# A two-layer decoder trunk on one core: norm steps in PSUM, four squares summed by TensorE, and four plain blocks in layer 1's second group

## The chip, the cores and the metric

The kernel runs on one core of a Trainium2 chip. The metric is the device time of one execution in microseconds (us). The core has a matrix engine (TensorE, PE in the profile, with PEld for its weight loads), a vector engine (VectorE, DVE), an activation engine (ScalarE, ACT), GpSimd (POOL) and SyncE (SP), which issues most of the DMA transfers. Each engine works through its own queue in order and waits there on semaphores of the others.

## The reference

One inference step of a trunk of two layers for 1024 prompt tokens and 64 sample tokens (8 requests of 8), all with the same weights. Model width is 1024, the channel mixer is 2816 wide, everything is float32.

```
for layer in (0, 1):
    hn  = rms_norm(h, norm_mix_g[layer])
    mix = conformer + stick-breaking attention   (layer 0)
          short gated convolution + causal pooling (layer 1)
    h   = h + mix
    g, u = split(rms_norm(h, norm_ffn_g[layer]) @ w_ffn_in[layer])
    h   = h + (silu(g) * u) @ w_ffn_out[layer]
y = rms_norm(h, norm_final_g)
rms_norm(x, g) = x * rsqrt(mean(x*x) + 1e-6) * g
```

Beside y, the new keys, values and convolution states are returned. The change lies in the norms and in layer 1's channel mixer (the last lines).

## The kernel before

**Layout and groups.** Activations are kept transposed: `hb` is [128, 8, 1088], 8 chunks (`n` or `k`) of 128 channels by 1088 token columns. Group A (`GA`) is columns 0 to 511 and four tiles of 128 tokens, group B (`GB`) is columns 512 to 1087 and five tiles (t = 4 to 8, the last half full). Every f32 product is made of three float32r products (high by high, high by low residual, low by high), so weights are split on the way in: ACT copies the high part (L187, L199), POOL subtracts it for the low part (L189, L200). `w_next` takes the next split weight tile `hl` (three buffers) and keeps the split up to two tiles and the loads up to four `stage` buffers ahead; SP issues the loads in the order of the list `seq`.

**Order of work.** The schedule is written by hand: each engine's queue has the order in which the Python emits. Side work is given out in slots between products: `slot()` is called at points inside a block and runs a step of a generator or pops a closure from a list.

**The norm.** `add_squares` squares a chunk on ACT (L254) and adds it to `ss` on POOL (L255); the first chunk is squared straight into `ss`. `norm_cols` lets TensorE add over the channels (L262: one token tile of `ss` is the weight, a column of ones the moving operand; each appears as two records), ACT takes the square root (L267), and DVE makes one Newton step for the reciprocal root with small [128, tiles] operations (L268 to L273) through the SBUF tiles `nw` and `rstd`. `norm_a` then multiplies an identity by `rstd` into `dg` (L279), `norm_b` spreads it over rows with a product by ones (L288) and ACT copies it to `rr` (L289).

**The channel mixer of layer 1.** `channel1` runs `run_ffn` for group A, then for group B. Each handles 22 column blocks f of 128 of the gate and the up half. The first `PLAIN1[group]` blocks are plain: `one(f, 0)` and `one(f, 1)`, each with 8 x 3 x 2 = 48 products of 288 columns for group B, 96 for the two. The others are done by `strassen(f)` with seven half-size products, 84 matmuls (L540) and additions on DVE (L544); four split weight tiles serve one f (sums of weight quarters on DVE, L203 to L205 and L217). In group A an output tile (`out_tile`, 24 matmuls of 512 columns at L238) follows each Strassen block from f = 2 on. Before: `PLAIN1 = (0, 1)`, so group A has no plain block and group B has one f, two plain blocks.

**The operands of the Strassen form.** They are combinations of quarters of the normed activations. For group A `forms_a` makes them while the mixer's output product of group B runs (`for n in range(KC)` with `block(GB, ...)` and `out_fin(GB, n, a)`, which adds to `hb` at L300 and calls `add_squares`). For group B `forms_b` is a generator run at every third slot of group A's channel blocks: `norm_a` at slot 3, `norm_b` at slot 9, and then the normed chunks into four tiles `xs[k]` (L1736). Once group A's products are done, `free_a` fills two lists:

- `seam`: eight pieces (ACT copy at L1840 and a low part on DVE at L1739, put off by the list `lowq`) and then the first two `job`s; `go_on` pops them in the slots of group A's last output products (`out_both`).
- `jobs`: the other two jobs, popped at every third slot of group B's plain blocks. `ready` runs what is left before the first Strassen block.

A `job(k)` makes four differences (L1743), three ACT copies (L1862) and three low parts (L1739). `last_part` cuts the last quarters after `out_both`. In group B's later slots `rows_a` squares, norms and writes group A's result. `to_y` and `finish` do the last output products of group B, its final norm in two parts (`norm_cols` for tiles 4 and 5, then 6 to 8 with `last7`) and the output.

Of the kernel before, what the change touches and what calls it, by code (L numbers as in the profile page):

```python
# [8 lines left out]
F = mybir.dt.float32  # L9
FR = mybir.dt.float32r  # L10
I32 = mybir.dt.int32
AF = mybir.ActivationFunctionType
OP = mybir.AluOpType
# [3 lines left out]
D = 1024  # L17
# [7 lines left out]
EPS = 1e-6  # L25
# [4 lines left out]
def f32(ap):  # L30
    return ap.bitcast(F)
# [14 lines left out]
GA = Grp(0, HALF, (0, 1, 512, 0))  # L46
GB = Grp(HALF, T, (0, 2, 288, 0))
# [10 lines left out]
def trunk_kernel(ctx, tc, x_prompt, x_sample, cache_k, cache_v, state_conformer, state_shortconv, state_pool,  # L58
# [4 lines left out]
    pe, act, dve, pool, sp = nc.tensor, nc.scalar, nc.vector, nc.gpsimd, nc.sync  # L63

    consts = ctx.enter_context(tc.tile_pool(name="consts", bufs=1))
# [12 lines left out]
    def tmp():  # L78
        return tmpbox[0].tile([128, tmpbox[1]], F, name="tmp")
# [4 lines left out]
    ones = consts.tile([128, 128], F, name="ones")  # L84
    dve.memset(ones, 1.0)
    eps = consts.tile([128, 1], F, name="eps")
# [3 lines left out]
    ss = consts.tile([128, 1152], F, name="ss")  # L90
    pool.memset(ss, 0.0)
    rr = consts.tile([128, T], F, name="rr")
    rstd = consts.tile([128, 9], F, name="rstd")
    nw = consts.tile([128, 2, 9], F, name="nw")
    hb = hpool.tile([128, KC, T], F, name="hb")
    park = dram.tile([128, KC, T], F, name="park")

# [39 lines left out]
            add_out(w_ffn_out[l], NF // 2 - 1, o)  # L137


    PLAIN, PLAIN1 = 5, (0, 1)  # L140


    EVEN = [(j, c) for c in range(4) for j in (0, 1, 2, 3)] + [(4, c) for c in range(4)]
# [105 lines left out]
    def add_squares(g, src, first):  # L249
        if first:  # L250
            act.activation(ss[:, g.cs], src, AF.Square)
            return
        t = tmp()
        act.activation(t[:, :g.n], src, AF.Square)  # L254
        pool.tensor_tensor(ss[:, g.cs], ss[:, g.cs], t[:, :g.n], op=OP.add)  # L255


    def norm_cols(ps, count, t0, t1, more=None):
        m = ps()
        c = slice(t0, t1)  # L260
        for t in range(t0, t1):
            pe.matmul(m[:, t:t + 1], ss[:, t * 128:t * 128 + 128], ones[:, 0:1], start=True, stop=more is None)  # L262
            if more is not None:
                pe.matmul(m[:, t:t + 1], more[:, (t - t0) * 128:(t - t0) * 128 + 128], ones[:, 0:1], start=False,
                          stop=True)
        r = rstd[:, c]
        act.activation(r, m[:, c], AF.Sqrt, bias=eps, scale=1.0 / count)  # L267
        dve.tensor_scalar(nw[:, 0, c], m[:, c], 1.0 / count, EPS, op0=OP.mult, op1=OP.add)  # L268
        dve.reciprocal(r, r)

        dve.tensor_tensor(nw[:, 1, c], nw[:, 0, c], r, op=OP.mult)
        dve.scalar_tensor_tensor(nw[:, 1, c], nw[:, 1, c], -0.5, r, op0=OP.mult, op1=OP.mult)
        dve.scalar_tensor_tensor(r, nw[:, 1, c], 1.5, r, op0=OP.add, op1=OP.mult)  # L273

    def norm_a(g, ps, count, dg=None):
        norm_cols(ps, count, g.t0, g.t1)
        k = g.t1 - g.t0
        dg = tmp() if dg is None else dg
        dve.tensor_tensor(dg[:, :k * 128].rearrange("p (t n) -> p t n", t=k),  # L279
                          ident[:, None, :].to_broadcast([128, k, 128]),  # L280
                          rstd[:, g.t0:g.t1, None].to_broadcast([128, k, 128]), op=OP.mult)
        return dg

    def spread(g, ps, src, scale):
# [6 lines left out]
    def norm_b(g, ps, dg):  # L291
        spread(g, ps, dg, 1.0)
# [5 lines left out]
    def added(g, dst, acc):  # L298
        for a, d in parts(g, acc, dst):
            dve.tensor_tensor(d, a, d, op=OP.add)  # L300
# [75 lines left out]
    lowq = []  # L376

    def low(n=0):
        while len(lowq) > n:
            lowq.pop(0)()  # L380
# [286 lines left out]
    def accs():  # L667
        return accbox["p"].tile([128, len(accbox["g"].blocks), 512], F, name="acc")

    def ms():  # L670
        return mp.tile([128, 512], F, name="m")
# [37 lines left out]
    m = ms()  # L709
# [838 lines left out]
    with tc.tile_pool(name="hid0b", bufs=2) as hidp:  # L1548
        fstack = ExitStack()
        fp = sums["p"] = fstack.enter_context(tc.tile_pool(name="forms", bufs=1))  # L1550
        forms, jobs = make_forms(GB, fp, FFNG)
# [178 lines left out]

    def out_fin(g, n, a):
        added(g, hb[:, n, g.cs], a)
        add_squares(g, hb[:, n, g.cs], n == 0)

    def normed(out, c, cs, view=lambda ap: ap):
        dve.scalar_tensor_tensor(out, view(hb[:, c, cs]), pc(FFNG + 8 + c), view(rr[:, cs]), op0=OP.mult, op1=OP.mult)  # L1736

    def lows(o, src):
        dve.tensor_tensor(o[:, 1], src, f32(o[:, 0]), op=OP.subtract)  # L1739

    def sums_t(b11, b12, b21, b22, t1, t2, t3, t4):
        for o, p, q in ((t1, b12, b11), (t3, b22, b12), (t2, b22, t1), (t4, b21, t2)):
            dve.tensor_tensor(o, p, q, op=OP.subtract)  # L1743
# [36 lines left out]
    a0, a1 = pair(GA, accs, xa, KS, {})  # L1780
    w_split(wj[0] + 3)
    out_fin(GA, 0, a0)
    out_fin(GA, 1, a1)
    todo_b = list(KS)

# [5 lines left out]
    for n in range(2, KC):  # L1791
        h = w_next()
        a = accs()
# [4 lines left out]
    with tc.tile_pool(name="fab", bufs=1) as ep:  # L1798
        gen = forms_a(ep)
        for n in range(KC):  # L1800
            h = w_next()
            a = accs()
# [14 lines left out]
    xs = [fp.tile([128, 2 * GB.n], F, name=f"xs{k}") for k in range(4)]  # L1817
    L, R = slice(0, W2), slice(W2, GB.n)
    seam, jobs, rest_b = [], [], {}


    def forms_b():
        dg = norm_a(GB, ms, D, xs[3])
        yield 1
        yield 1
        norm_b(GB, ms, dg)
        yield 1
        for k in range(4):
            normed(xs[k][:, 0:GB.n], k + 4, GB.cs)
            yield 1  # L1830
            normed(xs[k][:, GB.n:], k, GB.cs)
            yield 1

    def parts_b(k):
        return [xs[k][:, i * W2:i * W2 + W2] for i in range(4)]


    def free_a():
        def piece(o, i):
            act.activation(o[:, 0], i, AF.Copy)  # L1840
            low(1)
            lowq.append(lambda: lows(o, i))

        for k in range(4):
            seam.append(lambda k=k: piece(b2[k], xs[k][:, 0:GB.n]))
            seam.append(lambda k=k: piece(b1[k], parts_b(k)[2]))


        def last_part(k):
            if k == 0:  # L1850
                rest_b["t"] = hidp1.tile([128, 2, 2, GB.n], FR, name="hid").rearrange(
                    "p a s (b n) -> p (a s) b n", b=2)
            piece(rest_b["t"][:, k], parts_b(k)[3])

        def job(k):
            low()
            b21, b22, b11, b12 = parts_b(k)
            fast = k < 2
            t3 = b12 if k > 1 else fp.tile([128, W2], F, name="t3", bufs=2)
            sums_t(b11, b12, b21, b22, b11, b22, t3, b21)  # L1860
            for o, x in ((xa[k], xs[k][:, W2:3 * W2]), (xa[4 + k][:, :, R], t3), (xa[4 + k][:, :, L], b21)):
                act.activation(o[:, 0], x, AF.Copy)  # L1862
                if fast:
                    lowq.append(lambda o=o, x=x: lows(o, x))
                else:
                    lows(o, x)

        jobs.extend(lambda k=k: job(k) for k in range(4))
        seam.extend(jobs.pop(0) for _ in range(2))
        rest_b["f"] = last_part  # L1870

    def go_on():
        if len(lowq) > 2 or not seam:
            low(max(len(lowq) - 1, 0))
        elif seam:
            seam.pop(0)()
# [5 lines left out]
    def channel1(g, last, side, free, plain, x):  # L1882
        side = side()
        turn[0] = 0
        j0 = wj[0]

        def slot():
            turn[0] += 1
            if seam:
                return go_on()  # L1890
            if jobs and g is GB:
                if turn[0] % 3 == 0:
                    jobs.pop(0)()
            elif turn[0] % 3 == 0:
                if g is GA or wj[0] > j0 + 2 * plain + 2:
                    next(side, 0)

        def end(hh):
            if g is GB:
                for _ in side:  # L1900
                    pass
                fstack.close()
            last(hh)

        run_ffn(g, accs, ms, hidp1, x, end, slot=slot, forms=dict(form_views(g.n // 2), ready=ready), plain=plain,
                free=free, hw=GB.n, both=g is GA)
# [38 lines left out]
    def to_y(hh):  # L1945
# [44 lines left out]
        last7 = yp.tile([128, 384], F, name="last7")  # L1990
# [6 lines left out]
                sp.dma_start(y_p[0, t * 128:t * 128 + 128], y[:, t - 4])  # L1997

        def finish():
            norm_cols(ms, D, 6, 9, last7)  # L2000
            for t in range(6, 9):
                r = slice(0, 128 if t < 8 else 64)
                if t % 2:
                    act.activation(y[r, t - 4], y[r, t - 4], AF.Copy, scale=rstd[r, t:t + 1])
                else:
                    dve.tensor_scalar(y[r, t - 4], y[r, t - 4], rstd[r, t:t + 1], None, op0=OP.mult)
                if t < 8:
                    sp.dma_start(y_p[0, t * 128:t * 128 + 128], y[:, t - 4])
                else:
                    sp.dma_start(y_s.rearrange("b q c -> (b q) c"), y[:64, 4])  # L2010

        LAG = 2
        for q in range(16 + LAG):
# [6 lines left out]
            if q == 10:  # L2020
                norm_cols(ms, D, 4, 6)
        finish()

    channel1(GB, to_y, rows_a, lambda: None, PLAIN1[1],
# [40 lines left out]
```

## Time and profile before

| | |
|---|---|
| median of 3 runs | 2494.81 us (2493.42 to 2498.12) |
| profiled execution | 2494.09 us, its span 2492.3 us |
| TensorE busy (matmul) | 2415.4 us, 97% |
| DVE, ACT, POOL busy | 1625.9, 1104.3, 1617.5 us |
| granted TensorE clock, mean | 0.996 |

The span goes from the first to the last instruction. A row of a timeline is: start in us, length in us, engine, line of the source, operation, output<-inputs, shapes, count; in brackets the idle time of the engine before the row and what ended it. A busy TensorE row is modelled and says little of its speed, so starts are compared with starts. A group or tile row gives min/median/max or mean in ns. Rows of the chain that ended last are: start, length, engine, tile, line and count.

### The profile page before, as it was taken

To read this page: it belongs to the slowest core of one execution; us is meant where nothing else is said; L and a number is where in the kernel's file an instruction comes from. 1 tells how busy PE (TensorE), PEld (TensorE's weight loads), DVE (VectorE), ACT (ScalarE), POOL (GpSimd) and SP (SyncE) were. 2 spreads that over 40 slices of the span, in tenths; PEclk is the share of its full clock that TensorE was granted. 3 is DMA by queue.
4 is the path that set the end of the run, shared out by engine and by line. 5 is a ranking of instruction groups with operands and counts; after the bars stand their busy time and mean duration, and the time that the engine had idled before them with its cause. 6 is when DMAs were issued, how large, how long until landed. Compare 5 with 4: busy or idle time off the path is not lost.

```text
span 2492.3 us, 41476 instructions
## 1 busy us (share of the span) xinstructions
PE 2415.4 (97%) x15877; PEld 2188.2 (88%) x15877; DVE 1625.9 (65%) x2288; ACT 1104.3 (44%) x1877; POOL 1617.5 (65%) x1264
## 2 busy tenths in 40 slices
PE   8999999999999999999999999998999999999998
PEld 6788977788777679999999999888889988999998
DVE  3696878977777553766566533457666668666655
ACT  5535877754444343443333422234343344443333
POOL 6664344655554576787787523277888886887775
PEclk9999999999999999999999999999999999999999
DMA  7332241234665524223232311252333332233322
GB/s 224 113 109 75 76 123 43 72 111 137 179 181 169 161 90 152 77 69 100 87 98 85 113 52 43 61 150 62 92 102 102 100 96 85 85 102 113 92 85 81
DMA packets 355486, 258.32 MB, mean 104 GB/s; under 512 B 22913, under 2 KB 303617, under 8 KB 355272
## 3 DMA queue, kind: packets, MB, share of 16 engines
q1 hardware_dynamic: 355256, 255.66, 34.7%
q8 instruction: 126, 2.06, 0.3%
q14 instruction: 72, 0.59, 0.1%
q10 hardware_dynamic: 32, 0.01, 0.0%
HBM read 237.41 MB, written 18.69 MB: 103 GB/s over the span
## 4 chain that ended last, share of the span: by engine, by line
PE 75%; DVE 13%; POOL 5%; ACT 4%; issue 3%; DMA 1%; SPq 0%; DVEq 0%; ACTq 0%; POOLq 0%
PE acc L238 44%; PE acc L540 22%; POOL hl L200 2%; DVE q L1035 1%; DVE hb L300 1%; PE o L1057 1%; PE m L1159 1%; PE z L1182 1%; PE m L1047 1%; DVE cacc L858 1%; PE z L1018 1%; POOL hl L189 1%; DVE be L1037 1%; DVE sum L203 1%; DVE hid L244 1%
## 5 line engine op out<-in xcount | busy, mean ns | idle before, releaser
L189 POOL TENSOR_TENSOR hl<-stage,hl 128x512 fp32r<-128x512 f32 x464 | 638.6, 1400 | 391.6 <-ACT hl L187 279.9
L238 PE MATMUL acc<-x,hl 128*128 128x512 f32 (+1 forms) x3648 | 771.2, 349 | 11.3 <-DVE tmp L296 3.0
L238 PEld LDWEIGHTS acc<-x,hl 128*128 128x128 f32 x3648 | 585.6, 189 | 74.9 <-issue 5.8
L238 PE MATMUL acc<-hid,hl 128*128 128x288 f32 (+1 forms) x3096 | 542.1, 331 | 5.3 <-DVE hb L300 2.1
L238 PEld LDWEIGHTS acc<-hid,hl 128*128 128x128 f32 x3096 | 468.3, 189 | 51.0 <-DVE hb L300 4.2
L540 PE MATMUL acc<-x,hl 128*128 128x288 f32 (+1 forms) x2676 | 367.9, 291 | 7.9 <-POOL hl L200 3.7
L300 DVE TENSOR_TENSOR hb<-acc,hb 128x512 f32<-128x512 f32 (+1 forms) x360 | 255.5, 718 | 169.9 <-PE acc L238 168.6
L540 PEld LDWEIGHTS acc<-x,hl 128*128 128x128 f32 x2676 | 352.2, 189 | 14.1 <-POOL hl L200 7.0
L200 POOL TENSOR_TENSOR hl<-sum,hl 128x512 fp32r<-128x512 f32 x180 | 234.2, 1331 | 170.1 <-ACT hl L199 168.0
L187 ACT ACTIVATE hl<-stage 128x1024 fp32r<-128x1024 f32 x232 | 243.6, 1054 | 207.7 <-PE acc L238 141.4
L544 DVE TENSOR_TENSOR tmp<-acc,tmp 128x288 f32<-128x288 f32 (+1 forms) x420 | 174.4, 441 | 207.5 <-ACT tmp L556 102.1
L200 POOL TENSOR_TENSOR hl<-stage,hl 128x512 fp32r<-128x512 f32 x180 | 272.4, 1532 | 12.8 <-ACT hl L199 12.8
L540 PE MATMUL acc<-b,hl 128*128 128x256 f32 (+1 forms) x1548 | 216.0, 290 | 7.9 <-DVE tmp L544 5.8
L238 PE MATMUL acc<-x1t,hl 128*128 128x288 f32 x1152 | 216.3, 296 | 1.5 <-POOL hl L189 1.5
L540 PEld LDWEIGHTS acc<-b,hl 128*128 128x128 f32 x1548 | 201.7, 189 | 13.3 <-POOL hl L200 6.7
L238 PEld LDWEIGHTS acc<-x1t,hl 128*128 128x128 f32 x1152 | 195.9, 188 | 19.5 <-POOL hl L189 1.7
L199 ACT ACTIVATE hl<-sum 128x512 fp32r<-128x512 f32 x180 | 103.0, 623 | 187.5 <-DVE sum L205 164.6
L296 DVE TENSOR_TENSOR tmp<-acc,rr 128x512 f32<-128x512 f32 (+1 forms) x108 | 75.1, 710 | 128.1 <-PE acc L238 114.6
L199 ACT ACTIVATE hl<-stage 128x512 fp32r<-128x512 f32 x180 | 105.7, 619 | 70.4 <-PE acc L238 65.5
L507 POOL TENSOR_TENSOR tmp<-tmp 128x576 f32<-128x576 f32 (+1 forms) x85 | 124.3, 1462 | 9.2 <-ACT tmp L484 8.2
L238 PE MATMUL acc<-x1a,hl 128*128 128x512 f32 x480 | 122.6, 410 | 2.5 <-POOL hl L189 1.4
L255 POOL TENSOR_TENSOR ss<-ss,tmp 128x512 f32<-128x512 f32 (+1 forms) x69 | 106.3, 1541 | 25.9 <-ACT tmp L254 15.4
(299 smaller groups left out, 3129.6 us busy)
## 6 DMA issues: line engine op xcount, KB each, us to landing
stage<-in_w_ffn_in_dram SPq DMA_DIRECT2D x176, 512.0 KB
stage<-in_w_ffn_out_dram SPq DMA_DIRECT2D x88, 512.0 KB
stage<-in_w_in_even_dram SPq DMA_DIRECT2D x40, 512.0 KB
kst<-in_cache_k_dram SPq DMA_DIRECT2D x64, 256.0 KB
vst<-in_cache_v_dram SPq DMA_DIRECT2D x56, 256.0 KB
stage<-in_w_out_even_dram SPq DMA_DIRECT2D x16, 512.0 KB
stage<-in_w_in_odd_dram SPq DMA_DIRECT2D x16, 512.0 KB
stage<-in_w_out_odd_dram SPq DMA_DIRECT2D x16, 512.0 KB
```

Of the source, the lines that this page charges most:

```text
L187: act.activation(hl[:, 0], st, AF.Copy)
L189: pool.tensor_tensor(hl[:, 1, c], st[:, c], f32(hl[:, 0, c]), op=OP.subtract)
L199: act.activation(hl[:, 0, c], x, AF.Copy)
L200: pool.tensor_tensor(hl[:, 1, c], x, f32(hl[:, 0, c]), op=OP.subtract)
L203: todo = [lambda: dve.tensor_tensor(sb, su[:, lo], su[:, hi], op=OP.add), lambda: dve.tensor_tensor(sa[:, hi], sg[:, lo], su[:, lo], op=OP ...
L238: pe.matmul(acc[:, b, :c1 - c0], w, xs[:, xi, c0 - o:c1 - o], start=first and s == 0, stop=last and s == 2)
L255: pool.tensor_tensor(ss[:, g.cs], ss[:, g.cs], t[:, :g.n], op=OP.add)
L296: dve.tensor_tensor(d, a, r, op=OP.mult)
L300: dve.tensor_tensor(d, a, d, op=OP.add)
L507: (dve if both and f == NF - 1 else pool).tensor_tensor(t[:, :n], t[:, :n], u[:, :n], op=OP.mult)
L540: pe.matmul(acc[:, :w2], h[:, wi, i, k], xk[:, xi], start=k == 0 and s == 0, stop=k == 3 and s == 2)
L544: dve.tensor_tensor(out, acc[:, :w2], x, op=OP.add)
```

## The change

1. The tile `nw` goes. `norm_cols` is cut into `norm_sums` (TensorE's sums and the square root) and `norm_rest` (the DVE steps). The intermediate values of the DVE steps are held in columns of the PSUM tile `m` that holds the sums; where the diagonal is made (`norm_diag`), the result and the diagonal's second operand are in `m` too. The reciprocal stays in `rstd` in SBUF.
2. In the output product of layer 1's mixer, group B's chunks 4 to 7 are no longer squared and added in `out_fin`. In the first four slots of group A's channel blocks (f0 and f1) ACT squares each into an `xs[k]` of its own, POOL clears 64 columns behind it, and `norm_sums` lets TensorE add five weights per token tile (`ss` and four `xs`) instead of one.
3. `forms_b` makes the sums at slot 6 (the end of f2's Strassen block), the rest and the diagonal at slot 9, `norm_b` at slot 12 (the end of f3's Strassen block), so each later step comes three slots later.
4. `PLAIN1` is (0, 2): group B has four plain blocks (f0 and f1) and its first Strassen block is f2. All four jobs are run at every third slot of the plain blocks, none in the seam; their low parts follow the copies at once.

```diff
-    nw = consts.tile([128, 2, 9], F, name="nw")
...
-    PLAIN, PLAIN1 = 5, (0, 1)
+    PLAIN, PLAIN1 = 5, (0, 2)
...
-    def norm_cols(ps, count, t0, t1, more=None):
+    def norm_cols(ps, count, t0, t1, more=()):
+        m = norm_sums(ps, count, t0, t1, more)
+        norm_rest(m, count, t0, t1, rstd[:, t0:t1])
+
+    def norm_sums(ps, count, t0, t1, more=()):
         m = ps()
+        for t in range(t0, t1):
+            cs = [ss[:, t * 128:t * 128 + 128]] + [q[:, (t - t0) * 128:(t - t0) * 128 + 128] for q in more]
+            for i, q in enumerate(cs):
+                pe.matmul(m[:, t:t + 1], q, ones[:, 0:1], start=i == 0, stop=i == len(cs) - 1)
+        act.activation(rstd[:, t0:t1], m[:, t0:t1], AF.Sqrt, bias=eps, scale=1.0 / count)
+        return m
+
+    def norm_rest(m, count, t0, t1, out):
         c = slice(t0, t1)
...
-        dve.tensor_scalar(nw[:, 0, c], m[:, c], 1.0 / count, EPS, op0=OP.mult, op1=OP.add)
+        a, b, r = m[:, 16 + t0:16 + t1], m[:, 32 + t0:32 + t1], rstd[:, c]
+        dve.tensor_scalar(a, m[:, c], 1.0 / count, EPS, op0=OP.mult, op1=OP.add)
         dve.reciprocal(r, r)
-        dve.tensor_tensor(nw[:, 1, c], nw[:, 0, c], r, op=OP.mult)
-        dve.scalar_tensor_tensor(nw[:, 1, c], nw[:, 1, c], -0.5, r, op0=OP.mult, op1=OP.mult)
-        dve.scalar_tensor_tensor(r, nw[:, 1, c], 1.5, r, op0=OP.add, op1=OP.mult)
+        dve.tensor_tensor(b, a, r, op=OP.mult)
+        dve.scalar_tensor_tensor(b, b, -0.5, r, op0=OP.mult, op1=OP.mult)
+        dve.scalar_tensor_tensor(out, b, 1.5, r, op0=OP.add, op1=OP.mult)

     def norm_a(g, ps, count, dg=None):
-        norm_cols(ps, count, g.t0, g.t1)
+        return norm_diag(g, norm_sums(ps, count, g.t0, g.t1), count, tmp() if dg is None else dg)
+
+    def norm_diag(g, m, count, dg):
         k = g.t1 - g.t0
-        dg = tmp() if dg is None else dg
+        r = m[:, 48 + g.t0:48 + g.t1]
+        norm_rest(m, count, g.t0, g.t1, r)
         dve.tensor_tensor(dg[:, :k * 128].rearrange("p (t n) -> p t n", t=k),
                           ident[:, None, :].to_broadcast([128, k, 128]),
-                          rstd[:, g.t0:g.t1, None].to_broadcast([128, k, 128]), op=OP.mult)
+                          r[:, :, None].to_broadcast([128, k, 128]), op=OP.mult)
...
     def out_fin(g, n, a):
         added(g, hb[:, n, g.cs], a)
-        add_squares(g, hb[:, n, g.cs], n == 0)
+        if g is GA or n < 4:
+            add_squares(g, hb[:, n, g.cs], n == 0)
...
+    def square(k):
+        pool.memset(xs[k][:, GB.n:640], 0.0)
+        act.activation(xs[k][:, 0:GB.n], hb[:, 4 + k, GB.cs], AF.Square)
+
+    ahead1 = [lambda k=k: square(k) for k in range(4)]
+
     def forms_b():
-        dg = norm_a(GB, ms, D, xs[3])
+        m = norm_sums(ms, D, GB.t0, GB.t1, xs)
         yield 1
+        dg = norm_diag(GB, m, D, xs[3])
         yield 1
         norm_b(GB, ms, dg)
...
         def job(k):
...
-            fast = k < 2
...
-                if fast:
-                    lowq.append(lambda o=o, x=x: lows(o, x))
-                else:
-                    lows(o, x)
+                lows(o, x)
...
-        seam.extend(jobs.pop(0) for _ in range(2))
...
             if jobs and g is GB:
                 if turn[0] % 3 == 0:
                     jobs.pop(0)()
+            elif ahead1:
+                ahead1.pop(0)()
             elif turn[0] % 3 == 0:
```

More of the change, by code (lines that the diff above doesn't have):

```diff
@@ L255, in add_squares @@
         pool.tensor_tensor(ss[:, g.cs], ss[:, g.cs], t[:, :g.n], op=OP.add)
-    def norm_cols(ps, count, t0, t1, more=None):
+    def norm_cols(ps, count, t0, t1, more=()):
+        m = norm_sums(ps, count, t0, t1, more)
+        norm_rest(m, count, t0, t1, rstd[:, t0:t1])
+    def norm_sums(ps, count, t0, t1, more=()):
         m = ps()
-        c = slice(t0, t1)
[L261 to L267, printed above, removed]
-        dve.tensor_scalar(nw[:, 0, c], m[:, c], 1.0 / count, EPS, op0=OP.mult, op1=OP.add)
+        for t in range(t0, t1):
[4 more added lines that the diff above has]
+        return m
@@ L1999, in finish @@
         def finish():
-            norm_cols(ms, D, 6, 9, last7)
+            norm_cols(ms, D, 6, 9, [last7])
             for t in range(6, 9):
```

## The prediction

> **What bounds the kernel now.** I read the page's busy shares first, then the busy time by stretches, then the timelines of TensorE, GpSimd and VectorE inside the two stretches the change edits.
>
> ```profile
> PE 2415.4 (97%) x15877; PEld 2188.2 (88%) x15877; DVE 1625.9 (65%) x2288; ACT 1104.3 (44%) x1877; POOL 1617.5 (65%) x1264
> ```
> ```profile
> 1700.00:1780.00 80.00, 72.69 (x528) 68.56 (x528) 53.32 (x78) 35.48 (x60) 69.16 (x50) 0.98 0.29 83
> 2060.00:2094.00 34.00, 30.46 (x176) 26.69 (x176) 32.05 (x50) 14.73 (x29) 14.49 (x11) 1.00 0.21 62
> ```
> TensorE is busy 97% of the span, so an edit pays only where TensorE waits. Columns of the stretches: length, busy PE, PEld, DVE, ACT, POOL, clock, DMA. Layer 1's first channel group opens in 1700 to 1780: TensorE misses 7.3 us, and POOL is the fullest engine after it (69 of 80). The hand-over to the second group is 2060 to 2094: TensorE misses 3.5 us while DVE is full (32 of 34). Here is TensorE in the first stretch; the bracket is the wait before the row.
>
> ```profile
> 1707.56 3.21 PE L540 MATMUL acc<-x,hl 128*128 128x256 f32 x26
> ...
> 1715.79 1.44 PE L540 MATMUL acc<-x,hl 128*128 128x256 f32 x10 [1.66 <-POOL hl L200]
> ...
> 1720.12 1.45 PE L540 MATMUL acc<-b,hl 128*128 128x256 f32 x10 [0.92 <-POOL hl L200]
> 1721.41 2.98 PE L540 MATMUL acc<-x,hl 128*128 128x256 f32 x24
> ...
> 1733.93 2.41 PE L540 MATMUL acc<-b,hl 128*128 128x256 f32 x12 [2.74 <-DVE tmp L544]
> 1736.13 5.25 PE L540 MATMUL acc<-x,hl 128*128 128x256 f32 x36
> ...
> 1753.61 4.39 PE L540 MATMUL acc<-x,hl 128*128 128x256 f32 x36
> ...
> 1763.53 5.77 PE L238 MATMUL acc<-hid,hl 128*128 128x512 f32 x24
> 1769.14 4.43 PE L540 MATMUL acc<-x,hl 128*128 128x256 f32 x36
> ```
> Strassen blocks start at 1707.56 (f0), 1721.41 (f1), 1736.13 (f2) and 1753.61 (f3). f3 ran without a marked wait: 1763.53 - 1753.61 = 9.92 us for its 84 products, 15.53 with the output tile behind it. So f0 lost 13.85 - 9.92 = 3.93 us. f1 and f2 also held norm matmuls, 1.02 us each:
>
> ```profile
> 1724.39 1.02 PE m L262 x10
> ...
> 1751.29 1.02 PE m L288 x4
> ```
> f1 lost 14.72 - 9.92 - 1.02 = 3.78, f2 17.48 - 15.53 - 1.02 = 0.93; 8.64 us in the three.
>
> **The change, part by part.** *Four GpSimd additions go* (squares of chunks 4 to 7 into ss).
>
> ```profile
> 1701.49 1.88 POOL L255 TENSOR_TENSOR ss<-ss,tmp 128x576 f32<-128x576 f32 x1
> ...
> 1708.29 1.44 POOL L255 TENSOR_TENSOR ss<-ss,tmp 128x576 f32<-128x576 f32 x1
> ...
> 1712.18 1.89 POOL L255 TENSOR_TENSOR ss<-ss,tmp 128x576 f32<-128x576 f32 x1
> ...
> 1717.41 1.42 POOL L255 TENSOR_TENSOR ss<-ss,tmp 128x576 f32<-128x576 f32 x1
> ```
> ```profile
> L200 POOL TENSOR_TENSOR hl<-sum,hl 128x512 fp32r<-128x512 f32 x180 | 234.2, 1331 | 170.1 <-ACT hl L199 168.0
> ...
> L200 POOL TENSOR_TENSOR hl<-stage,hl 128x512 fp32r<-128x512 f32 x180 | 272.4, 1532 | 12.8 <-ACT hl L199 12.8
> ```
> ```profile
> L1991 POOL MEMSET last<- 128x64 f32 x1 | 0.2, 152 | 0.0
> ```
> ```profile
> L1743 DVE TENSOR_TENSOR xs<-xs x14: 443/459/1532, 2069.4 to 2091.8; 128x288 f32<-128x288 f32 x14
> ```
> That is 6.63 us off POOL's queue, each addition between the weight splits (L200) that f0 waits for; four 64-column memsets at 0.15 come instead. What is late next? POOL writes seven splits per block, four from sums and three from stage: 4 x 1.33 + 3 x 1.53 = 9.9 us, and one gate product, taken like a split, 1.3: 11.2 against TensorE's 9.92. f0's first pair of splits ended at 1708.29, where the second row starts, so it began near 1705.3. A sum beside the 1701.49 row is no longer stretched (by up to 1.1, the shortest and longest of the L1743 row, a difference of two SBUF operands), so the pair can begin near 1704.2, 3.3 us ahead of TensorE; an estimate. That lead lasts through f1 and runs out at f2's third tile, about 1.1 us late. With slot waits I take 1.5 us left of the 8.64; ends 0 (lead holds) and 5.9 (only f1's 2.74 goes). The four Squares only move on ACT, which is busy 35 of 80.
>
> *The norm chain on DVE leaves f1 and its steps go to PSUM.* f1's 2.74 us wait is an accumulator's release behind this chain:
>
> ```profile
> 1726.03 0.74 DVE L271 TENSOR_TENSOR nw<-nw,rstd 128x5 f32<-128x5 f32 x1
> 1726.81 1.22 DVE L272 SCALAR_TENSOR_TENSOR nw<-nw,rstd 128x5 f32<-128x5 f32 x1
> 1728.06 1.21 DVE L273 SCALAR_TENSOR_TENSOR rstd<-nw,rstd 128x5 f32<-128x5 f32 x1
> 1729.31 1.88 DVE L279 TENSOR_TENSOR xs<-ident,rstd 128x640 f32<-128x640 f32 x1
> ```
> ```profile
> 1009.02 0.17 DVE L271 TENSOR_TENSOR nw<-nw,rstd 128x5 f32<-128x5 f32 x1
> ...
> 1009.69 0.83 DVE L279 TENSOR_TENSOR tmp<-ident,rstd 128x640 f32<-128x640 f32 x1
> ```
> ```profile
> L544 DVE TENSOR_TENSOR tmp<-acc,tmp x420: 408/447/460, 1088.2 to 2449.7; 128x288 f32<-128x288 f32 x89, 128x256 f32<-128x256 f32 x51
> ```
> The same steps take 0.17 and 0.83 elsewhere: the long ones have two SBUF inputs and lie beside GpSimd work. L544, with one input in PSUM, never passed 0.46 in 420 calls. After the edit each step has at most one SBUF input, so I cost the chain at 3 x 0.17 + 0.83 = 1.34 instead of 5.05. It also moves behind f2, inside an output tile whose 5.6 us of products cover it.
>
> [...]
>
> The other norms gain as little: TensorE has products queued beside them. Each holds its PSUM bank about 1.6 us longer; with no cover that would cost at most 1.6 each, and no wait stands there now. A write into PSUM is bounded by
>
> ```profile
> L858 DVE SCALAR_TENSOR_TENSOR cacc<-ext,par,cacc x100: 745/756/757, 95.7 to 190.9; 128x512 f32<-128x512 f32 x100
> ```
> ```profile
> 2072.12 0.68 DVE L300 TENSOR_TENSOR hb<-acc,hb 128x512 f32<-128x512 f32 x1
> ```
> about 0.08 us more than the 0.68 of an addition of that width into SBUF (the second row). Two norms at the end of the kernel lie on the path, three such steps each: between 0 and 0.4, I take +0.3.
>
> *TensorE adds the four squares.* Five tiles of tokens times five matmuls, where there were five: the ten records above took 1.02, so fifty take 5.10, +4.08 us, placed between f2's products and its output tile. Nothing covers it. It does let POOL and DVE run ahead by up to three weight tiles, and the row-spread matmuls now follow f3, which gives f4 the same.
>
> ```profile
> 1785.41 4.39 PE L540 MATMUL acc<-x,hl 128*128 128x256 f32 x36
> ```
> f4, from 1769.14 to here, took 16.27 against f3's 15.53; of these 0.74 I take back 0.4 (0 to 0.7).
>
> *The jobs leave the seam for the second group, and one more f is plain.*
>
> ```profile
> 2286.85 22.32 PE acc L540 x168
> 2309.17 12.80 PE acc L238 x96
> ```
> Two Strassen blocks are 22.32; 96 products of the plain form 12.80. One more plain f costs 12.80 - 11.16 = +1.64 on TensorE. Against it stand the seam's waits:
>
> ```profile
> 2072.86 4.48 PE L238 MATMUL acc<-hid,hl 128*128 128x512 f32 x18 [1.85 <-DVE hb L300]
> ...
> 2092.57 0.40 PE L540 MATMUL acc<-x,hl 128*128 128x288 f32 x1 [1.30 <-ACT x L1862]
> 2093.36 3.73 PE L540 MATMUL acc<-x,hl 128*128 128x288 f32 x26 [0.39 <-DVE x L1739]
> ```
> ```profile
> 2064.62 4.84 DVE L1739 TENSOR_TENSOR b<-xs,b 128x576 fp32r<-128x576 f32 x4
> ...
> 2083.11 3.99 DVE L1743 TENSOR_TENSOR xs<-xs 128x288 f32<-128x288 f32 x4
> ...
> 2092.55 1.50 DVE L1739 TENSOR_TENSOR x<-xs,x 128x576 fp32r<-128x576 f32 x3 [0.26 <-ACT x L1862]
> ```
> The addition shown at 2072.12, for which TensorE waited 1.85, stood behind the first job; without jobs it follows the row that ends at 2069.46, so the 1.85 goes. The 18 products behind it ended near 2077.2, so the plain stage then starts near 2075.3 and lasts 2 x 12.8 = 25.6 us, to 2100.9; the last operand is needed about 1 us later. Jobs 2 and 3 ran from 2083.11 to 2094.05, 5.5 us each, while Strassen weights were split beside them. A job without GpSimd beside it is about 3.7 (four differences at 0.44 by the L1743 row, lows 0.75 + 2 x 0.45, 0.26 for ACT). DVE can start them near 2077.8, behind the last addition to hb (near 2076) and four lows of 0.45. Its other work there is some 5.6 us, estimated as four gate products and lows at 0.75 and three weight sums at 0.7 to 1: the end is 2098 at 3.7 a job and 2105 at 5.5, a stall of 0 to 3.5. The plain stage splits fewer weights per us, so I lean to the short end and take 1.0. Net: -1.85 - 1.69 + 1.0 + 1.64 = -0.90 us. The row work of the second group starts at the same block f2 as now, on POOL and SP too, so I cost that at nothing.
>
> **The sum.** -(8.64 - 1.5) + 4.08 - 0.4 - 0.9 + 0.3 = -4.06 us. The profiled execution took 2494.09 (span 2492.3), 0.7 under the median 2494.81. On the median: 2490.7.
>
> **Rivals.**
> - *Nothing is left of the waits.* Lead and jobs both hold, PSUM steps cost nothing: -8.64 + 4.08 - 0.7 - 1.9 = -7.2, 2487.6. For it: 6.0 us leave POOL's queue where f0's waits name POOL. Against: POOL still needs 11.2 us for blocks of 9.92.
> - *The sums' products pay for little.* POOL's waits in f0 and f2 stay, since DVE's sums for the next block are slowed by back-to-back splits, and only f1's 2.74 goes: -2.74 + 4.08 - 0.4 - 0.9 + 0.3 = +0.3, 2495.1.
> - *The PSUM steps stay long*: the change does not do what it says, because their stretch comes from rstd, which stays in SBUF. The chain of 5.05 us then stalls an accumulator in f2's output tile for the 2.74 again: -1.3, 2493.5. L544's flat 0.46 speaks against it.
> - *Slower: the jobs overrun the plain blocks.* Place: the first Strassen block of the second group. If GpSimd's splits fall beside the differences, one takes up to the 1.53 of the L1743 row, not 0.44. Each us more per job delays TensorE by 4. The gain is gone at a stall of 5.1 us, a mean job of 5.9; at 7.5 a job DVE ends at 2077.8 + 30 + 5.6 = 2113.4, a stall of 11.5, net +6.4, 2501.2. The measured 5.5 beside a fuller POOL speaks against it.
>
> **Numbers.** Main forecast 0.40, no waits left 0.27, sums pay for little 0.15, PSUM steps long 0.09, jobs overrun 0.09. About 0.2%, 5.0 us, is what a measurement of this kernel can tell from no change. Faster by more: the first rival and the main case's edge, 0.27 + 0.06 = 0.33. Slower by more: 0.09. Within: 0.58. Range 2487.5 to 2496: from the first rival to just above the second; it leaves out the overrun and the edges. The likeliest case's own range is 2489 to 2493.
>
> **What the profile after would show.** f0 near 10 us and f1 within a us of that; 50 norm records of 5.1 us after f2; the four steps at 0.17 and 0.83 with one PSUM operand; no wait for hb at the seam; four plain blocks at 6.4 us, and at most a us or two before the first Strassen product. It is wrong if f0 or f1 still loses over 2 us, if the 50 records cost other than 5 us, or if DVE's jobs end past 2103.

## The result, and the profile after

| | before | after |
|---|---|---|
| median | 2495.49 us (6 runs) | 2481.99 us (6 runs, 2479.66 to 2484.60) |
| profiled execution | 2494.09, span 2492.3 | 2479.66, span 2477.9 |
| granted clock, mean | 0.996 | 0.993 |

The ratio is 0.9948 [0.9938, 0.9959]: the changed kernel is 0.5% faster, 13.5 us by the medians. The forecast was 2490.7, with a range that ended at 2487.5. The page's first lines, and the two stretches of the prediction's second fence, moved to where the same work now lies (11 us earlier, and 8.5 us earlier):

```profile
PE 2408.3 (97%) x15929; PEld 2194.9 (89%) x15929; DVE 1616.8 (65%) x2278; ACT 1102.0 (44%) x1871; POOL 1604.7 (65%) x1260
```
```profile
1689.00:1769.00 80.00, 77.64 (x555) 74.08 (x554) 51.24 (x75) 36.09 (x61) 63.04 (x49) 0.94 0.28 80
2051.50:2085.50 34.00, 34.00 (x213) 31.47 (x212) 29.15 (x40) 13.12 (x23) 16.57 (x12) 1.00 0.28 80
```
TensorE misses 2.4 us of the first stretch instead of 7.3 and nothing of the second instead of 3.5. That looks like the forecast, and more. Two things in it do not: the clock column of the first line is 0.94, not 0.98, and both edited stretches together cannot yield 13.5 us. Lining up the matmuls of the two traces that have the same line, tile and order, and taking the difference of their starts, tells where the time went:

| start in before, us | 240 | 660 | 900 | 1140 | 1380 | 1680 | 2160 | 2460 |
|---|---|---|---|---|---|---|---|---|
| after minus before, us | -1.1 | -3.6 | -5.8 | -8.1 | -9.5 | -10.9 | -12.6 | -14.7 |

At 1680, ahead of all edited work but the norms, 10.9 us are already won. They come a little at a time, over every stretch with wide products. (Two single traces can differ by some us without an edit: each has short falls of the granted clock at other places, above all between 200 and 1100 us, where its mean was 0.99 in these two and 0.98 in the padded kernel of experiment 1, which lies 3.3 us behind before at 1680. So what counts below is how a difference changes across a stretch.) Here is the first edited stretch on TensorE, after:

```profile
1696.53 4.47 PE L548 MATMUL acc<-x,hl 128*128 128x256 f32 x36
...
1706.56 4.48 PE L548 MATMUL acc<-x,hl 128*128 128x256 f32 x36
...
1717.12 4.48 PE L548 MATMUL acc<-x,hl 128*128 128x256 f32 x36
...
1728.02 0.28 PE L266 MATMUL m<-ones,ss 128*128 128x1 f32 x2
...
1730.18 0.36 PE L266 MATMUL m<-ones,ss 128*128 128x1 f32 x2
1730.40 1.64 PE L266 MATMUL m<-ones,xs 128*128 128x1 f32 x8
1731.90 0.57 PE L266 MATMUL m<-ones,ss 128*128 128x1 f32 x2
...
1736.17 7.92 PE L237 MATMUL acc<-hid,hl 128*128 128x512 f32 x24
1743.92 4.48 PE L548 MATMUL acc<-x,hl 128*128 128x256 f32 x36
```
f0 takes 10.03 us, f1 10.56 and f2's products 10.90, near the 9.92 of a block without waits. But the sums run from 1728.02 to 1736.17, 8.15 us where 5.10 were forecast: the first two token tiles take 1.1 us each, the third 1.7, the last two 2.1. The 24 output products behind them take 7.75 us; those of the next block take 5.57. The same places by granted clock (columns as in the windows above):

```profile
1728.00:1730.00 2.00, 2.00 (x21) 2.00 (x19) 2.00 (x5) 0.50 (x1) 1.60 (x1) 1.00 0.05 19
1730.00:1731.00 1.00, 1.00 (x9) 1.00 (x10) 1.00 (x3) 0.13 (x1) 0.00 (x0) 0.81 0.15 44
1731.00:1731.50 0.50, 0.50 (x4) 0.50 (x4) 0.35 (x1) 0.04 (x1) 0.00 (x0) 0.50 0.76 208
...
1733.00:1740.00 7.00, 7.00 (x25) 6.23 (x26) 0.69 (x1) 2.21 (x4) 4.52 (x5) 0.50 0.01 2
1740.00:1741.50 1.50, 1.50 (x6) 1.18 (x6) 0.12 (x1) 0.00 (x0) 0.96 (x1) 0.71 0.00 0
```
The 0.81 of the second line puts the fall at about 1730.6: 2.6 us into the row of one-column products the clock falls to 0.50 and stays there for some 10 us. Nothing in the prediction allowed for it.

So two theories had to be told apart. *Theory of the steps*: the time comes from the edited stretches, as forecast, in some larger size. *Address theory*: the tile `nw` is gone, every later tile on the left side of SBUF lies 96 bytes lower (its 72 bytes are rounded up), and the products run faster for that. In the compiled program the split weights `hl` start at 44864 before and 44768 after; `x1_0`, on the right side, stays at 192480. Over all 512-column products the median step from one start to the next fell from 234 to 227 ns.

### The profile page after: what moved, and what is told of

It reads as the page before. It is cut to its first block, busy times and chain, and to the rows that moved or that the text cites. A ratio compares the mean times of both kernels' runs of the same rounds, so it can differ in the third digit from the quotient of the medians.

```text
span 2477.9 us, 41552 instructions
## 1 busy us (share of the span) xinstructions
PE 2408.3 (97%) x15929; PEld 2194.9 (89%) x15929; DVE 1616.8 (65%) x2278; ACT 1102.0 (44%) x1871; POOL 1604.7 (65%) x1260
## 4 chain that ended last, share of the span: by engine, by line
PE 74%; DVE 9%; POOL 4%; ACT 3%; issue 3%; DMA 0%; SPq 0%; DVEq 0%; ACTq 0%; POOLq 0%
PE acc L237 43%; PE acc L548 23%; POOL hl L199 2%; DVE q L1043 1%; POOL hl L188 1%; PE o L1065 1%; PE m L1167 1%; PE m L1055 1%; PE z L1026 1%; PE z L1190 1%; DVE hb L308 1%; DVE be L1045 1%; PE m L266 1%; POOL tmp L515 1%; DVE kt L1003 1%
## 5 line engine op out<-in xcount | busy, mean ns | idle before, releaser
L237 PE MATMUL acc<-x,hl 128*128 128x512 f32 (+1 forms) x3648 | 764.9, 348 | 10.2 <-ACT hl L186 3.1
L548 PE MATMUL acc<-x,hl 128*128 128x288 f32 (+1 forms) x2628 | 359.9, 291 | 3.4 <-DVE tmp L552 2.3
L548 PE MATMUL acc<-b,hl 128*128 128x256 f32 (+1 forms) x1512 | 209.8, 290 | 4.4 <-DVE tmp L552 3.3
L548 PEld LDWEIGHTS acc<-b,hl 128*128 128x128 f32 x1512 | 196.5, 189 | 9.3 <-POOL hl L199 5.0
L515 POOL TENSOR_TENSOR tmp<-tmp 128x512 f32<-128x512 f32 (+1 forms) x84 | 122.8, 1462 | 9.2 <-ACT tmp L492 8.2
L243 DVE TENSOR_TENSOR hid<-tmp,hid 128x576 fp32r<-128x576 f32 (+1 forms) x66 | 79.5, 1207 | 64.0 <-ACT hid L242 64.0
```

What stands on the lines that cost most here:

```text
L237: pe.matmul(acc[:, b, :c1 - c0], w, xs[:, xi, c0 - o:c1 - o], start=first and s == 0, stop=last and s == 2)
L243: (on or dve).tensor_tensor(dst[:, 1], src, f32(dst[:, 0]), op=OP.subtract)
L515: (dve if both and f == NF - 1 else pool).tensor_tensor(t[:, :n], t[:, :n], u[:, :n], op=OP.mult)
L548: pe.matmul(acc[:, :w2], h[:, wi, i, k], xk[:, xi], start=k == 0 and s == 0, stop=k == 3 and s == 2)
```

## The experiments

All edits are small. "Distance" below is the address of the next weight tile minus that of the current moving operand, modulo 256, the same for all but some fifty of the 512-column products of a kernel (addresses from the compiled program, steps from start times in the trace). Where differences of starts are given, they are between two traces as in the table above.

**1. Dead bytes: is it the address?** The changed kernel with 96 dead bytes where `nw` was, and three kernels with 32 dead bytes: before with them behind `nw`, the changed kernel with them on the left, and on both sides.

```diff
     rstd = consts.tile([128, 9], F, name="rstd")
+    consts.tile([128, 18], F, name="pad")          # first kernel: 72 bytes, rounded to 96
+    consts.tile([128, 8], F, name="pad")           # the others: 32 bytes; in before, behind nw
+    ctx.enter_context(tc.tile_pool(name="rpad", bufs=1, side="right")).tile([128, 8], F, name="rpad")  # fourth
```

> The changed kernel with a dead tile where nw stood, so that every tile behind it in SBUF has the address that it had before the change. Address theory: the 10.9 us that the changed kernel is ahead by 1690 us, ahead of all edited work but the norms, come from the 96 bytes by which the split weights hl moved; here the 512-column products go back from 227 to 234 ns a step and the time is 2490 to 2494 us. Theory of the steps (the norm chains in PSUM give it): the time stays at 2480 to 2484 and the step stays 227.

> The kernel before the change with 32 dead bytes more behind nw; nothing else differs, hl goes from 0 to 32 modulo 64, as x1 stands. Address theory: the 512-column step is 227 ns and the time falls by 8 to 13 us, to 2482 to 2488. Theory of the steps: 2494 to 2497, as before.

> The changed kernel with 32 dead bytes in nw's place: hl at 0 modulo 64, x1 at 32. Address theory, if it is the remainder modulo 64: slow step of 234 ns and 2490 to 2494 us, like 96 bytes. If it is some larger period, the step is 227 and the time 2480 to 2484. Theory of the steps: 2480 to 2484.

> The changed kernel with 32 dead bytes on each side of SBUF: hl, hb and the left side at 0 modulo 64, x1, tmp and the right side at 0 too. Address theory, if it takes equal remainders of weights and moving operand: step 227, 2480 to 2484 us. If it takes weights at 32 modulo 64: step 234, 2490 to 2494. Theory of the steps: 2480 to 2484.

The padded changed kernel took 2491.20 us, ratio 0.9987 [0.9977, 0.9996] to before, with steps of 234 ns: at equal addresses the change is worth 3.8 us by the medians and the rest of the 13.5 is the 96 bytes. The three others, at distances of 128, 32 and 64, took 2491.80, 2489.96 and 2486.96; their steps are 232, 233 and 233 ns. None has the 227. So the first form of the address theory, a remainder modulo 64, is out: by it the second kernel would have had 227 ns and 2482 to 2488 us.

**2. The removal of `nw` alone, and the same 96 bytes on the other side.** The first kernel ("PSUM steps alone" below) is before with the norm steps in PSUM, and with one thing more of the change: the DVE steps and the diagonal come one step of `forms_b` behind the sums, at slot 6 and not at slot 3; the sums stay at slot 3 and `norm_b` at slot 9. It has no squares moved, no block more and no job moved. The second is the changed kernel with the right side's tiles moved down by 96 bytes as well.

```diff
+    ctx.enter_context(tc.tile_pool(name="rpad", bufs=1, side="right")).tile([128, 24], F, name="rpad")
     x1p = x1stack.enter_context(tc.tile_pool(name="x1b", bufs=1, side="right"))
```

> Of the change only the norm steps in PSUM (and with them the loss of the tile nw, so that every later tile on the left lies 96 bytes lower, as in the changed kernel); squares, plain blocks and jobs as before. Address theory (the step of the 512-column products hangs on the distance of the next weight tile's address to the moving operand's, modulo 256, and is shortest at 0): steps of 227 ns as in the changed kernel, and about 9 us less than before, 2484 to 2488. Theory of the steps (the time comes from the norm chains and the second group's blocks): at most 0.5 us less than before, 2494 to 2496, steps of 234 ns.

> The changed kernel whole, with 96 dead bytes ahead of the tiles on the right side, so that the operands there lie 96 bytes lower too, while the weights stay at the changed kernel's addresses. If the distance between weights and moving operand counts, it is 96 modulo 256 again as before: steps of 233 to 235 ns and 2489 to 2493. If the weights' own address counts: steps of 227 ns and 2480 to 2484.

The first took 2483.79 us, ratio 0.9962 [0.9949, 0.9976], with steps of 227 ns. By the starts it is 9.9 us ahead at 1680, which its addresses give, and wins another 1.8 across the first group's opening, where the chain moved. The changed kernel with the right side moved took 2492.61, 0.9989 [0.9980, 0.9998], steps of 234 ns, although every weight stays at its fast address. So it is the distance that counts. (Distance 96 was reached from either side, distance 0 at one pair of addresses only; before's own medians beside these runs were 2494.3 to 2495.5.)

| distance | kernels | median step, ns | medians, us |
|---|---|---|---|
| 0 | after; PSUM steps alone | 227, 227 | 2482.0, 2483.8 |
| 32 | after + 32 bytes left | 233 | 2490.0 |
| 64 | after + 32 bytes left and right | 233 | 2487.0 |
| 96 | before; after + 96 left; after + 96 right | 234, 234, 234 | 2495; 2491.2; 2492.6 |
| 128 | before + 32 bytes left | 232 | 2491.8 |

Read straight from the trace: the same 74 products at the seam, in the changed kernel, padded on the left, and moved on the right.

```profile
2049.22 17.07 PE L237 MATMUL acc<-hid,hl 128*128 128x512 f32 x74 [0.72 <-DVE hid L243]
```
```profile
2061.91 17.60 PE L238 MATMUL acc<-hid,hl 128*128 128x512 f32 x74 [0.72 <-DVE hid L244]
```
```profile
2057.70 17.60 PE L238 MATMUL acc<-hid,hl 128*128 128x512 f32 x74 [0.72 <-DVE hid L244]
```
17.07 / 74 is 231 ns, 17.60 / 74 is 238. Over the some 2,770 recorded steps the mean falls by 4.6 ns (235.1 to 230.5, steps over 260 ns counted as 260), 12.8 us together; the starts of the right-moved kernel fall behind the changed one's by 9.9 us at 1680 and 12.9 at the end. The medians give 9.2 and 10.6.

**3. The sums, spread.** The five token tiles' sums one by one, first in five slots in a row (popped from `ahead1` behind the squares), then in every third slot, which is shown; then in two rows, of three token tiles and of two (one `yield` between them).

```diff
-        m = norm_sums(ms, D, GB.t0, GB.t1, xs)
+        m = ms()
+        for t in range(GB.t0, GB.t1):
+            sum_tile(m, t, GB.t0, xs)      # five products, one token tile
+            yield 1                        # three slots
+        sums_root(m, D, GB.t0, GB.t1)
```

> The changed kernel, with the 25 sums not in a row but one token tile's five (ten records) in each of five slots in a row: one behind f2's products, four between the output products behind them. Clock theory (50 one-column records in a row let TensorE's granted clock fall to a half, and the price beyond 5.1 us is that): clock at 1.0 throughout, the sums 5.1 us together, the output products at 5.6, about 4 to 5 us less than the changed kernel, 2477 to 2478.5. If some 1.4 us of products between the sums aren't enough to keep the clock, or if the records are slow for another reason: 2481 to 2483.

> The same with the five sums in every third slot, so that 4 us or more of products stand between two of them; the norm's end comes 12 slots later. Clock theory: clock at 1.0 throughout and 2476.5 to 2478.5. If the records are slow by themselves: 2481 to 2483. If the later norm makes the operands of the second group late: a wait at the seam and 2480 or more.

> The changed kernel with the sums in two rows: three token tiles (30 records) behind f2's products, two (20 records) three slots later. Clock theory: the granted clock fell 2.8 and 3.4 us into the row of 50, so a row of 3.06 us stands at the edge: without a fall 2476 to 2478, with a short one behind the first row 2478 to 2481. If it takes spreading by single token tiles: the clock at a half over 10 us as in the changed kernel, 2481 to 2483.

One by one in five slots: 2476.33 us, 0.9931 [0.9918, 0.9945]. In every third slot: 2475.06, 0.9921 [0.9907, 0.9934], the fastest kernel here. The instructions are the same; the clock over the whole stretch of sums is now 1.00 (five slots in a row):

```profile
1730.66:1741.68 11.02, 11.02 (x76) 10.01 (x75) 6.17 (x12) 3.52 (x7) 7.85 (x6) 1.00 0.18 54
```
The 24 output products and 50 records take 11.02 us; in the changed kernel 15.90. Group rows of the sums, spread in every third slot and then in the changed kernel (ns, min/median/max):

```profile
L271 PE MATMUL m<-ones,xs x40: 250/250/250, 1735.6 to 1771.9; 128*128 128x1 f32 x40
```
```profile
L266 PE MATMUL m<-ones,xs x40: 250/352/353, 1728.2 to 1736.0; 128*128 128x1 f32 x40
```
In two rows it took 2479.68, 0.9949 [0.9936, 0.9963] (2477.89 to 2486.24), between the others, and its profiled execution, of 2485.27, has the fall, 2.1 us into the first row: the first row of 30 records, then the 18 products behind it.

```profile
1733.13:1737.48 4.35, 4.35 (x32) 4.35 (x31) 3.32 (x7) 1.54 (x3) 1.71 (x2) 0.74 0.36 102
1737.48:1743.81 6.33, 6.33 (x20) 5.03 (x21) 1.38 (x2) 2.56 (x4) 6.10 (x5) 0.64 0.05 15
```
So a row of 30 records, some 3.06 us by the 1.02 of ten, could be enough for the fall (0.74 in the first line); rows of 1 us with 1.4 us of wide products between them were not (1.00 above).

**4. One part undone.** Both kernels stay at the changed kernel's addresses. The squares undone: `out_fin` adds all eight squares on GpSimd again, `norm_sums` gets no `xs`. As the four slots of the squares (`ahead1`) go too, each step of `forms_b` comes three slots earlier than in the changed kernel: sums at slot 3, DVE steps at 6, `norm_b` at 9. The last part undone: `PLAIN1 = (0, 1)`, two jobs in the seam, the low parts of these two put off.

```diff
-        if g is GA or n < 4:
-            add_squares(g, hb[:, n, g.cs], n == 0)
+        add_squares(g, hb[:, n, g.cs], n == 0)
...
-        m = norm_sums(ms, D, GB.t0, GB.t1, xs)
+        m = norm_sums(ms, D, GB.t0, GB.t1)
...
-    ahead1 = [lambda k=k: square(k) for k in range(4)]
+    ahead1 = []
```
```diff
-    PLAIN, PLAIN1 = 5, (0, 2)
+    PLAIN, PLAIN1 = 5, (0, 1)
...
-                lows(o, x)
+                if k < 2:
+                    lowq.append(lambda o=o, x=x: lows(o, x))
+                else:
+                    lows(o, x)
...
+        seam.extend(jobs.pop(0) for _ in range(2))
```

> The changed kernel at its own addresses with the four squares undone: GpSimd adds all eight squares again, and TensorE sums 5 columns of one operand (10 records) and not 25. By the prediction's terms (8.64 - 1.5 of waits come back, 4.08 of sums go): about 3 us more than the changed kernel, 2484 to 2486. By the traces (the sums cost some 9.5 with the clock's fall, the waits gave about 8.5): 2480 to 2482, no fall of the clock, waits for POOL in f0 to f2 again.

> The changed kernel at its own addresses with the last part undone: three plain blocks in the second group, two of the four operand jobs back in the seam, and the split lows put off for these two. By the prediction's terms (-0.90 for the second seam): 0.9 us more than the changed kernel, 2482.5 to 2483.5. By the traces of the padded kernel and of before (the second seam gave 3.7 us): 2485 to 2487, with the wait for hb at the seam back and 74 products no longer in a row. If four plain blocks cost what they save: 2481 to 2482.5.

With these two, the changed kernel and the PSUM steps alone, there is a table of four at the same addresses (medians; ratios to before in brackets):

| | three plain blocks, two jobs in the seam | four plain blocks |
|---|---|---|
| GpSimd adds all squares | 2483.79 (0.9962) | 2478.41 (0.9940) |
| four squares summed by TensorE | 2487.02 (0.9968) | 2481.99 (0.9948) |

The last part is worth 5.0 to 5.4 us by the medians and some 4 to 5 by the starts from 2040 to 2160. The squares, with their slots, cost 3.2 to 3.6 by the medians; by the ratios, each to before in its own session, only 1.5 to 2.0, and the intervals overlap. The starts are clearer: from 1680 to 1800, across the first group's opening, they move by +3.1 us in either column. Without the squares the kernel is faster than the 2480 to 2482 expected from the traces; by the prediction's terms it should have been slower.

Where the squares' gain went is seen in the kernel without them, whose waits in f0 to f2 are:

```profile
1702.05 1.46 PE L548 MATMUL acc<-x,hl 128*128 128x256 f32 x10 [0.19 <-POOL hl L199]
...
1706.80 1.45 PE L548 MATMUL acc<-x,hl 128*128 128x256 f32 x10 [1.64 <-POOL hl L199]
...
1711.13 1.45 PE L548 MATMUL acc<-b,hl 128*128 128x256 f32 x10 [0.93 <-POOL hl L199]
...
1722.91 1.45 PE L548 MATMUL acc<-b,hl 128*128 128x256 f32 x10 [0.36 <-POOL hl L199]
...
1733.58 1.69 PE L548 MATMUL acc<-b,hl 128*128 128x256 f32 x12 [0.62 <-DVE tmp L552]
```
The products of f0 to f2 take 38.34 us before, 35.49 here and 31.49 in the changed kernel. Before's 2.74 us wait on VectorE is gone here too, without the squares: the norm chain now comes three slots behind the sums, with its steps in PSUM. Only 4.0 us are the squares' own. Against them stand 7.1 us more of sums and some 2.2 us of output products at half clock, 5.3 net; some 2 of these come back, as f2's output tile takes 0.9 us longer in the kernel without the squares, and f4 and f5 together 1.1.

**5. The norm steps back in SBUF.** The padded changed kernel, with `nw` in place of the dead bytes.

```diff
-        a, b, r = m[:, 16 + t0:16 + t1], m[:, 32 + t0:32 + t1], rstd[:, c]
+        a, b, r = nw[:, 0, c], nw[:, 1, c], rstd[:, c]
```

> The changed kernel with the norm steps in SBUF as before, the tile nw back in its place and so all addresses as before. Beside the padded changed kernel (2491.2) this is the PSUM steps alone, without their effect on addresses. Prediction and address theory: within 1 us of the padded kernel, 2490 to 2492.5, steps of 234 ns. If the PSUM steps by themselves had made the gain: 2494 or more.

2491.91 us, 0.9989 [0.9980, 0.9998], beside 2491.20 and 0.9987 with the steps in PSUM: no difference that can be measured. From f0's start to f6's it takes 95.82 us, the padded kernel 95.70. For this place the PSUM columns are not what made the chain short, as its rows with the steps in SBUF show:

```profile
1755.10 0.17 DVE L277 TENSOR_TENSOR nw<-nw,rstd 128x5 f32<-128x5 f32 x1
1755.30 0.17 DVE L278 SCALAR_TENSOR_TENSOR nw<-nw,rstd 128x5 f32<-128x5 f32 x1
1755.50 0.17 DVE L279 SCALAR_TENSOR_TENSOR rstd<-nw,rstd 128x5 f32<-128x5 f32 x1
1755.70 0.83 DVE L288 TENSOR_TENSOR xs<-ident,rstd 128x640 f32<-128x640 f32 x1
```
```profile
1751.14 1.28 POOL L516 TENSOR_TENSOR tmp<-tmp 128x512 f32<-128x512 f32 x1
1756.45 3.01 POOL L200 TENSOR_TENSOR hl<-stage,hl 128x512 fp32r<-128x512 f32 x2 [4.02 <-ACT hl L199]
```
In its new slot the chain meets an idle GpSimd. What the PSUM operand is worth beside a busy one shows only in the two kernels with the chain at slot 6, PSUM steps alone and squares undone. In the first, whose rows follow, a split starts at 1738.46 under the diagonal. The diagonal still takes 0.82, where the one with two SBUF operands had taken 1.88 before:

```profile
1738.39 0.82 DVE L287 TENSOR_TENSOR xs<-ident,m 128x640 f32<-128x640 f32 x1
```
```profile
1738.46 3.76 POOL L199 TENSOR_TENSOR hl<-sum,hl 128x512 fp32r<-128x512 f32 x3 [2.65 <-ACT hl L198]
```

## Why the prediction was wrong, step by step

**A step that was missing: the addresses.** The prediction began with "an edit pays only where TensorE waits" and costed what is removed with `nw` as instructions and operands, not as 96 bytes. These are worth 9.2 us by the padded kernel and 10.6 by the right-moved one, more than any term of the sum, and they come from products that wait for nothing. With the addresses held, the change took 2491.20, half a us from the forecast, but by luck: two of its terms were wrong in opposite directions. By the starts, the opening cost 1.3, the second seam gave 3.7 and the end cost 0.4: -2.0 together, inside the ratio's interval of 1.0 to 5.7 us won.

**f0 to f2: right in size.** Forecast 8.64 - 1.5 = 7.14 us of waits gone; measured 38.34 - 31.49 = 6.85. f0 is 10.03, f1 10.56. Of this, 2.85 us came with the chain's later place (and its steps in PSUM) and 4.0 from the squares. But not all of the 8.64 were waits. Behind the 2.74 us wait the granted clock had fallen in before, too (the 0.98 in the prediction's second fence):

```profile
1734.00:1738.00 4.00, 4.00 (x21) 4.00 (x22) 2.96 (x6) 3.72 (x7) 4.00 (x4) 0.57 0.01 4
```
So f2's first 36 products took 5.25 us where f3's took 4.39. That is nearly all of the 0.93 that the prediction put down as f2's loss. The two kernels with the chain at slot 6 have neither the wait nor a fall there.

**The sums: the term that failed.** Forecast +4.08 at "ten records took 1.02, so fifty take 5.10", which the spread kernels confirm at a full clock. In one row they took 8.15 and slowed the output products from 5.6 to 7.75: some +9.3 in place of +4.08. The prediction carried a price over from a short row to one five times as long, with the clock assumed to stay; with the sums spread the clock stayed and the price held. Records at other than 5 us were one of the prediction's own signs of being wrong. From f0's start to f6's start, before took 94.41 us, after 95.91, the padded kernel 95.70 and the sums in every third slot 90.20: the first group's opening lost 1.3 to 1.5 us where 3.5 were to be won, and with the sums spread it wins 4.2. The 0.4 taken back at f4 came as 0.76 (f4 took 15.51 with its output tile).

**The second seam: right in kind, a quarter of its size.** Forecast -0.90; the starts of the padded kernel against before give -3.7 between 2040 and 2160, the table of four 5.0 to 5.4 at the changed addresses. The row of output products shortens by 2.1 (forecast 1.85), and the plain block costs 12.75 less a Strassen block of 11.19, 1.56 (forecast 1.64). The rest differs. The first two Strassen blocks had lost 2.4 us before, where the prediction took 1.69 from the brackets; 2.3 of it went. The stall that was taken at 1.0 does not come. In the changed kernel VectorE's last job ends just behind the start of the first Strassen block (2091.57):

```profile
2086.02 1.48 DVE L1748 TENSOR_TENSOR x<-xs,x 128x576 fp32r<-128x576 f32 x3
...
2088.10 1.92 DVE L1752 TENSOR_TENSOR xs<-xs 128x288 f32<-128x288 f32 x4
2090.28 1.50 DVE L1748 TENSOR_TENSOR x<-xs,x 128x576 fp32r<-128x576 f32 x3 [0.26 <-ACT x L1877]
```
The last operand is ready at 2091.78 and needed about a us behind the block's start. And a wait that the prediction left out went too: behind the next row of output products TensorE lost 0.83 us on VectorE (L544) before, 0.4 after and nothing in the padded kernel; that closes the sum to -3.7. With the last part undone the seam's wait for `hb` is back:

```profile
2070.01 6.00 PE L237 MATMUL acc<-hid,hl 128*128 128x512 f32 x18 [2.17 <-DVE hb L308]
```
Here the 18 products behind the wait took 6.00 us, 4.48 before: the granted clock fell again (0.57 in 2070 to 2074), as it did in the kernel PSUM steps alone (0.57 in 2063 to 2067) and not in before. These 1.5 us are part of what the last part is worth more at the changed addresses.

**The PSUM steps.** The durations were right (0.16 to 0.18, 0.82), but in the changed kernel the later place alone gives them, as the steps in SBUF show. What PSUM steps would do in the old place, at slot 3, no run here shows. In the first edited stretch that changes no number. The +0.3 at the end of the kernel fits: from 2400 to the end of its span the padded kernel loses 0.4 us on before, and the one with the steps in SBUF nothing. A PSUM source cost the steps no time that shows: beside an idle GpSimd such a step took 0.15 to 0.18 us in either memory.

**The rivals.** None was right. The jobs did not overrun, the steps did not stay long, and the case "sums pay for little" names the right place with the wrong reason: the waits went, and the sums took the gain.

## What to carry to other kernels

A tile added or removed moves all that lies behind it, so compare an edit at equal addresses (dead bytes in the tile's place) before its time is put down to the edit; and where TensorE is busy 97% of the span, try a few offsets between weights and moving operands, because 96 dead bytes were worth more here than a careful rearrangement. Narrow products that followed one another for 2.1 to 3.4 us let the granted clock fall to 0.50, and the wide products behind them paid (7.75 us for 24 in place of 5.57); hand them out one token tile at a time between wide ones, which here turned a loss of about 3 us against the kernel without them into a gain of 2 to 3. When work leaves a queue, look whether a neighbouring move had already freed the wait.

## What the runs showed of the hardware

**Step of wide products and addresses.** 512-column products with a new weight tile each step at 227 ns where weight and moving operand start a multiple of 256 bytes apart, and at 232 to 234 ns at distances of 32, 64, 96 and 128. The narrower products follow other orders over the same runs: with 288 columns 131 ns at 0 and 133 at 128, with 256 columns 120 at 0 and 114 at 64. So no offset is best for all, which may be why the kernel at distance 64 took 2487.0 with its wide products at 233. 160 to 224 bytes were not tried for 512 columns, and why the step hangs on where the two lie, by 5 to 7 ns of 230, stays open.

**Clock under narrow products.** TensorE was busy without a gap (7.00 of the 7.00 us from 1733 in the changed kernel), yet the granted clock fell to 0.50 after 2.6 us of one-column fp32 products in the changed kernel, 3.4 in the padded one and 2.1 in the two-row one (this last worked out from the 0.74 over 4.35 us). In the first two it stayed there for 10.2 us, the second half of them wide products; in the third for 6.8 (from the same 0.74 and the 0.64 over 6.33 us), and behind the 2.74 us wait in before for 3.4 (0.57 over 4 us). What lowers the clock in a queue full of one-column products no run here shows; that they follow one another in a row does count: the same products, spread, left the clock at 1.00.
